# A hybrid RWKV-7 and short-convolution block: weight casts moved in a scheduler's order, splits of mixed activations spread over projection tiles

## The chip, the core and the metric

The kernel runs on one core of a Trainium2 chip. A core has five engines that take their instructions in order, each from its own stream: TensorE (PE, matrix products, with its weight loads shown as PEld), VectorE (DVE), ScalarE (ACT), GpSimd (POOL) and SyncE (SP), which here issues nearly all DMAs, one after another from one queue. The metric is the device time of one execution in microseconds; lower is better.

## What is computed

One layer of a streaming encoder over 16 meta tokens and 512 tokens of width 2048, in float32. The reference, cut to its course:

```python
hn = _rmsnorm(h_res, norm_in_g[l])
P = hn @ w_in[l]                          # 2048 -> 8320 columns
Pr, Pc = P[..., :RW_COLS], P[..., RW_COLS:]
prev = jnp.pad(Pr[:, :-1], ((0, 0), (1, 0), (0, 0)))
Pr = Pr + (prev - Pr) * mu_shift[l]       # token shift; then r, k, v, g_r, wl, al
w_raw = -jax.nn.softplus(-(w0[l] + jnp.tanh(wl) @ w_lora_up[l])) - 0.5
decay = jnp.exp(-jnp.exp(w_raw))
a = jax.nn.sigmoid(a0[l] + al @ a_lora_up[l])
# kk: k * k_k, normalised by head; k = k * (1 + (a - 1) * k_a)
y = _rwkv7_recurrence(rh, decay, kh, vh, kk, kk * ah)     # 16 heads x 64
y_a = (group_norm(y) + bonus) * jax.nn.silu(g_r)
y_b = Bg * _causal_depthwise_conv(Cg * hc, conv_w[l]) * jax.nn.silu(g_c)
h_res = h_res + jnp.concatenate([y_a, y_b], axis=-1) @ w_out[l]
out = _rmsnorm(h_res, norm_f_g)[:, N_META:]
```

## The kernel before, in words

**Precision.** Both large projections are made of three products of rounded halves: a float32 operand is split into a rounded high part (a cast on ACT) and the rest (a subtraction on DVE or POOL), and PE adds high x high, low x high and high x low. `split_w` (L123) does this to a weight quarter of 128x512: the cast of L126 on ACT (`wh`), the subtraction of L127 (`wl`), on DVE for even quarters and on POOL for odd ones. `hi` and `lo` have six buffers each, the raw weights (`wr`, 512 KB, two quarters) three. `prefetch` (L130) issues the load on SP (L134) and the two splits.

**The projection.** `plan` lists 65 tiles of 128 output columns: the low-rank tile, then for each pair of heads i its k, r, v and g, and for each channel block C, h, B and gc. `main` (L322) makes one tile from four weight quarters: 96 matmuls, or 48 of twice the width for B and gc (L314). `mains` (L448) is a generator of all tiles in turn, `use` (L376) evicts a finished tile and does what follows from it (token shift, gate, the convolution: L391 to L419, whose results for channel block i go to the DRAM tile `mixd[8 + i]`).

**The order of PE is written by hand** (L79). All other work of the recurrence is placed between projection matmuls: `fill(ns)` (L500) advances the generator by so many nominal nanoseconds, `until` (L510) until a tile is there, `step` (L491) by one matmul. The FW table (L43) holds the amounts. The other engines' orders are made by the scheduler of the language from the order of recording, dependencies and a priority; `tc.high_priority(offset=n)` makes what is recorded under it rank n places earlier. `ahead` (L532) and `low_rank` use an offset of AHEAD = 600. Stores and loads that wait for a later time are kept by `later` and issued by `run_pending`.

**A pair's preparation.** `prepare(i)` (L568) takes pair i's k, low-rank and r tiles. `low_rank` gives tz and ta (tanh on ACT); L580 adds 1 to tz on DVE, L582 is a running sum (`cc`), L584 and L586 exponentials; L589 to L609 make the operands bk and ar and the product r; L614 to L616 split a square and r (casts L550 on ACT, L551 on DVE); the gram matmuls L624 follow, masked from PSUM by L633; L653 transposes; L663 to L670 sums. Then SP stores and loads re-tiled blocks, and DVE solves 16x16 triangular blocks by many small steps (L699 to L732: `prod`, `tt`, `y`). The solved blocks are stored by L747 and loaded again by L738 and L739. `invert` (L770) joins two pairs' blocks.

**The recurrence.** `recur` (L873) walks nine chunks for all eight pairs, with projection tiles of the last channel blocks between its steps; `norm` (L950) normalises a chunk and stores it to the DRAM tile `yd`.

**The end.** `split_mix(j)` (L996) makes the two halves of mixed tile j, the left operand of the output projection. For j below 8 it loads three pieces from DRAM (L1003 to L1007), combines them on DVE (L1010, two instructions) and splits: cast on ACT (L1015), subtraction on DVE (L1016). For j of 8 and above it loads `mixd[j]` (L1014) and splits. The raw tile has four buffers, the other two pieces three each. In the kernel before, `recur` is followed by `fill(14000)`, the remaining stores, and all 16 calls in a row; for j of 8 and above, the generator is first advanced until that block's gc tile is there (L1018 to L1022). What then remains of the projection, the last B and gc tiles among it, runs to its end, and the output projection begins (L1054): four column blocks of 512, each over 16 mixed tiles and four token blocks, then residual, norm and the stores.

Of the kernel before, what the change touches and what calls it, by code (L numbers as in the profile page):

```python
# [13 lines left out]
ALU = mybir.AluOpType  # L14
# [6 lines left out]
KT = DM // P  # L21
# [6 lines left out]
NPAIR = 8  # L28
# [13 lines left out]

FW = dict(  # L43
    evac=34, start=1062, lora=2200, gram=8000, gram_b=13500, gram2=4800, gram3=3500, misc=2000, v=2000, vt=1000, solve=22500, solve_first=26000,
    tr=3200, lev=3000, cp=4200, out=1500, begin=17000, p=2900, u=2900, s=5200, last=14000,
)


AHEAD = 600


def _constants():
# [24 lines left out]
def hymba_kernel(ctx: ExitStack, tc: tile.TileContext, xt, xtok, w_in, w_out, pv, lup, cst, msk, gf, out):  # L77
    nc = tc.nc
    ctx.enter_context(tc.manual_schedule(engines={mybir.EngineType.PE}))  # L79
    cp = ctx.enter_context(tc.tile_pool(name="cp", bufs=1))  # L80
# [16 lines left out]
    def col(off, i=0):  # L97
        return pvt[:, off + i : off + i + 1]
# [24 lines left out]
    def split_w(q, rq, eng):  # L123
        hi = wp.tile([P, 512], F32R, tag="hi", name=f"wh{q}", bufs=6)
        lo = wp.tile([P, 512], F32R, tag="lo", name=f"wl{q}", bufs=6)
        nc.scalar.copy(hi, rq)  # L126
        eng.tensor_tensor(out=lo, in0=rq, in1=hi.bitcast(F32), op=ALU.subtract)  # L127
        quarters[q] = (hi, lo)

    def prefetch(upto):  # L130
        while state["next"] < min(upto, len(stream)):
            j = state["next"]
            raw = wp.tile([P, 1024], F32, tag="raw", name=f"wr{j}", bufs=3)
            state["dma"] = nc.sync.dma_start(raw, stream[j]).ins  # L134
            for q in range(2):
                split_w(2 * j + q, raw[:, q * 512 : (q + 1) * 512], nc.gpsimd if q and j > 8 else nc.vector)
            state["next"] = j + 1

    keep = ctx.enter_context(tc.tile_pool(name="keep", bufs=1, side="right"))
# [21 lines left out]
    def tr(name, dt=F32):  # L161
        return cq.tile([P, LP], dt, tag="tr", name=name, bufs=5)
# [14 lines left out]
    raw = {}  # L177
# [80 lines left out]
    with tc.issue_after(head):  # L258
        load_w(0, 1)
        load_x("gt0", 4, 4)  # L260
        load_w(1, 1)
        load_w(2, 1)
        state["next"] = 3
        load_x("gt1", 8, 4)
        for kt in range(4, 8):
            split_x(kt)
        for kt in range(4):
            square_x(kt)
        prefetch(5)
        load_x("bk", 12, 3)  # L270
        load_x("v", 15, 1)
        for kt in range(8, KT):
            split_x(kt)
            square_x(kt - 4)
        for kt in range(KT - 4, KT):
            square_x(kt)
# [4 lines left out]
    for b in range(2):  # L281
# [5 lines left out]
        out=omm, in0=pvt[:, V_MU : V_MU + 33], scalar1=-1.0, scalar2=1.0, op0=ALU.mult, op1=ALU.add  # L287
    )
    for d, off in (
# [4 lines left out]
            out=d, in0=pvt[:, off : off + 8], scalar1=0.5, scalar2=None, op0=ALU.mult  # L294
        )
    nc.vector.tensor_scalar(
        out=hv[:, 4], in0=pvt[:, V_KA : V_KA + 8], scalar1=-0.5, scalar2=1.0, op0=ALU.mult, op1=ALU.add
# [24 lines left out]
    def main(j, ranges, name):  # L322
        prefetch(2 * j + 4)
        ps = banks(ranges, name, pm, "main")
        for k4 in range(4):
            if k4 == 1:
                prefetch(2 * j + 5)
            yield from steps(ps, ranges, k4, 4 * j + k4)
        return ps
# [92 lines left out]
    ready = set()  # L422
# [62 lines left out]
    def run_pending(upto):  # L485
        while pending and pending[0][0] <= upto:
            fn = pending.pop(0)[1]
            with tc.issue_after(state["dma"]):
                fn()

    def step():  # L491
        t = next(flow, None)
        if t is None:
            run_pending(float("inf"))
        else:
            clock[0] += t
            run_pending(clock[0])
        return t

    def fill(ns):  # L500
        while ns > 0:
            seen = len(ready)
            t = step()
            if t is None:
                return
            ns -= t
            if len(ready) > seen:
                ns += FW["evac"]
# [5 lines left out]
    def low_rank(i, j, up, w0, name, pad):  # L514
        t = tr(name)
        nc.gpsimd.memset(t[:, META:CH], pad)
        hi, lo = up
        for a, b in ((0, 272), (272, L)):
            z = pz.tile([P, b - a], F32, tag="tz", name=f"{name}_{a}")
            nc.tensor.matmul(z, hi[:, j], la[:, j, a:b], start=True, stop=False)  # L520
            nc.tensor.matmul(z, lo[:, j], la[:, j, a:b], start=False, stop=True)
            with tc.high_priority(offset=AHEAD):
                if a == 0:
                    nc.scalar.activation(t[:, 0:META], z[:, 0:META], AF.Tanh, bias=w0, scale=0.5)
                    nc.scalar.activation(t[:, CH : 5 * CH], z[:, META:272], AF.Tanh, bias=w0, scale=0.5)
                else:
                    nc.scalar.activation(t[:, 5 * CH : LP], z, AF.Tanh, bias=w0, scale=0.5)
            fill(FW["lora"])
        return t


    def ahead():  # L532
        return tc.high_priority(offset=AHEAD)

    def c3(t):
        return t.rearrange("p (c s) -> p c s", s=CH)
# [31 lines left out]
    def prepare(i):  # L568
        p = i % 2
# [7 lines left out]

        tz = low_rank(i, 0, up, hv[:, 0, i : i + 1], f"tz{i}", -1.0)
        ta = low_rank(i, 1, up, hv[:, 1, i : i + 1], f"ta{i}", 0.0)
        nc.vector.tensor_scalar(out=tz, in0=tz, scalar1=1.0, scalar2=None, op0=ALU.add)  # L580
        cc = tr(f"cc{i}")
        nc.vector.tensor_tensor_scan(cc, smask.rearrange("p c s -> p (c s)"), tz, 0.0, op0=ALU.mult, op1=ALU.add)  # L582
        nc.gpsimd.memset(e1[:, :, 0:1], 1.0)
# [7 lines left out]
            out=bk[:, :, 0], in0=c3(k), scalar=hv[:, 2, i : i + 1], in1=c3(te), op0=ALU.mult, op1=ALU.mult  # L591
# [3 lines left out]
            out=ta, in0=ta, scalar1=hv[:, 3, i : i + 1], scalar2=hv[:, 4, i : i + 1], op0=ALU.mult, op1=ALU.add  # L595
        )
        nc.vector.scalar_tensor_tensor(
            out=ar[:, :, 0], in0=c3(k), scalar=col(V_KK, i), in1=e1[:, :, 0:CH], op0=ALU.mult, op1=ALU.mult
# [8 lines left out]
            out=ar[:, 1:NCH, 1], in0=c3(r), in1=e1[:, 1:NCH, 1 : CH + 1], op=ALU.mult  # L607
        )
        nc.vector.scalar_tensor_tensor(  # L609
            out=r, in0=r, scalar=hv[:, 5, i : i + 1], in1=ta[:, CH:LP], op0=ALU.mult, op1=ALU.mult  # L610
# [98 lines left out]
        def sub(x, r0, c0, dims):  # L709
            return bass.AP(tensor=x.tensor, offset=x.offset + r0 * 16 + c0, ap=[list(x.ap[0])] + dims)  # L710

        for m in (2, 4, 8):
            for b in range(16 // (2 * m)):
# [4 lines left out]
                    out=pq,  # L718
                    in0=sub(d, o, o + m, [[16, m], [0, m], [1, m]]),
# [4 lines left out]
                    out=tq.rearrange("p (i j) -> p i j", i=m), in_=pq, op=ALU.add, axis=AX.X  # L724
                )
                nc.vector.tensor_tensor(
                    out=pq,
                    in0=sub(y, o, o, [[16, m], [0, m], [1, m]]),
# [254 lines left out]
    for i in range(0, NPAIR, 2):  # L983
        invert([prepare(i), prepare(i + 1)])
    until("g", NPAIR - 1)
    ph2.close()
    with tc.tile_pool(name="ch", bufs=1, side="right", reuse_waits="tile") as ch:
        recur(ch)
        fill(FW["last"])
        run_pending(float("inf"))  # L990

    pp = ctx.enter_context(tc.tile_pool(name="pp", bufs=1, side="right", reuse_waits="tile"))
    order = list(range(KT))
    parts = {}

    def split_mix(j):  # L996
        parts[j] = [pp.tile([P, SEQ], F32R, name=f"m{a}{j}") for a in range(2)]
        mh, ml = parts[j]
        raw = pp.tile([P, SEQ], F32, tag="mraw", name=f"mr{j}", bufs=4)
        if j < NPAIR:  # L1000
            rb = pp.tile([P, SEQ], F32, tag="rb", name=f"rb{j}", bufs=3)
            gg = pp.tile([P, SEQ], F32, tag="gg", name=f"gg{j}", bufs=3)
            nc.sync.dma_start(rb, rbd[j])  # L1003
            nc.sync.dma_start(gg, gated[j])
            for h, hs, ho in heads:
                o = (h * NPAIR + place[j]) * CH
                nc.sync.dma_start(raw[hs], yd[o : o + CH])  # L1007

            for x, w, z, o in ((raw, 0, rb, ALU.mult), (raw, 1, gg, ALU.add)):
                nc.vector.scalar_tensor_tensor(  # L1010
                    out=raw, in0=x, scalar=hl[:, w, j : j + 1], in1=z, op0=o, op1=(ALU.add, ALU.mult)[w]
                )
        else:
            nc.sync.dma_start(raw, mixd[j])  # L1014
        nc.scalar.copy(mh, raw)  # L1015
        nc.vector.tensor_tensor(out=ml, in0=raw, in1=mh.bitcast(F32), op=ALU.subtract)  # L1016

    for j in order:  # L1018
        if j >= NPAIR:
            while ("gc", j - NPAIR) not in ready:  # L1020
                step()
        split_mix(j)  # L1022
    for _ in flow:
        pass
# [10 lines left out]
    last = [[pw.tile([P, 512], F32R, name=f"wlast{a}{j}") for j in range(NL)] for a in range(2)]  # L1035
# [105 lines left out]
    with tc.manual_schedule(engines={mybir.EngineType.DVE, mybir.EngineType.Activation, mybir.EngineType.Pool}):  # L1141
# [9 lines left out]
        for part in range(2):  # L1151
# [3 lines left out]
            if part == 0:  # L1155
                finish(2)
                nc.vector.tensor_tensor(
                    out=fv[:, 3, 0:1], in0=fv[:, 3, 0:1], in1=ssq[:, 3, 3:4], op=ALU.add
# [60 lines left out]
```

## Time and profile before

| | us |
|---|---|
| median of 3 runs (1066.67 to 1069.53) | 1066.87 |
| the profiled execution | 1066.87 |
| its span in the profile | 1065.1 |
| PE busy | 1040.0 |
| DVE busy | 557.2 |
| ACT busy | 367.7 |
| POOL busy | 292.4 |
| output projection begins | 877.66 |

The profile shows one execution. Lines such as L127 are those of the kernel before. A row of a timeline gives start, duration, engine, line, operation, result and operands with the shape, the count, and in brackets how long the engine stood idle just before and what ended it. A row of the chain of waits gives start, duration and what ran; the chain is followed back from the last instruction to what released each step. A row of the waits names who waited for whom, the total in microseconds, how often, and the longest. "Granted clock" is the share of TensorE's full clock that the throttle allowed.

### The profile page before, as it was taken

The page shows a single profiled execution, that of the slowest core. Times are in us where ns is not written, and L with a number is a line of the kernel's source. Part 1 is how long each engine was busy: PE and PEld are TensorE (multiplying, and loading weights), DVE is VectorE, ACT ScalarE, POOL GpSimd, SP SyncE. Part 2 cuts the span into 40 slices and gives each one's busy share as a digit, 9 for nine tenths or more (in the row PEclk, how much of TensorE's full clock was granted, in tenths as well). Part 3 has the DMA queues.
Part 4 walks back from the last instruction along what each step waited for, and adds up shares of the span by engine and source line. Part 5 has one row for each costly group of instructions (what it writes and reads, how often), then busy time and mean ns, then how long its engine had stood idle before and what let it go on. Part 6 is the DMA issues. An engine that isn't in the chain of part 4 may idle for free.

```text
span 1065.1 us, 23993 instructions
## 1 busy us (share of the span) xinstructions
PE 1040.0 (98%) x9973; PEld 950.0 (89%) x9973; DVE 557.2 (52%) x1064; ACT 367.7 (35%) x682; POOL 292.4 (27%) x307
## 2 busy tenths in 40 slices
PE   8999999999999999999999999999999899999996
PEld 6999998999998999989999989898898878888885
DVE  6784964758553767644676552355444842212132
ACT  6553422533233443233443232222222342323232
POOL 0121323223132222231222231323223142424232
PEclk9999999999999999999999999999999999999999
DMA  8455564455653366643457638676745958333314
GB/s 291 137 136 138 142 169 133 128 132 144 172 152 113 107 169 145 147 141 112 124 127 173 176 108 312 215 243 188 224 104 147 244 184 315 82 96 99 99 60 158
DMA packets 182894, 167.49 MB, mean 157 GB/s; under 512 B 120961, under 2 KB 143233, under 8 KB 182401
## 3 DMA queue, kind: packets, MB, share of 16 engines
q1 hardware_dynamic: 182208, 164.90, 54.7%
q8 instruction: 78, 1.28, 0.5%
q10 hardware_dynamic: 576, 1.07, 0.3%
q14 instruction: 32, 0.25, 0.1%
HBM read 129.05 MB, written 36.88 MB: 156 GB/s over the span
## 4 chain that ended last, share of the span: by engine, by line
PE 91%; DVE 3%; DMA 2%; issue 1%; ACT 1%; SPq 0%; POOL 0%; DVEq 0%; ACTq 0%; POOLq 0%
PE o L1054 17%; PE ps_g L314 9%; PE ps_k L314 9%; PE ps_B L314 8%; PE ps_r L314 8%; PE ps_v L314 8%; PE ps_h L314 8%; PE ps_C L314 8%; PE ps_gc L314 8%; PE g L624 2%; PE zs L932 1%; PE zy L936 1%; DVE mr L1010 1%; PE rz L887 1%; PE ps_lora L314 1%
## 5 line engine op out<-in xcount | busy, mean ns | idle before, releaser
L127 POOL TENSOR_TENSOR wl<-wr,wh 128x512 fp32r<-128x512 f32 x150 | 209.3, 1398 | 486.2 <-ACT wh L126 456.5
L126 ACT CAST wh<-wr 128x512 fp32r<-128x512 f32 x312 | 189.4, 619 | 417.9 <-PE o L1054 92.5
L127 DVE TENSOR_TENSOR wl<-wr,wh 128x512 fp32r<-128x512 f32 x162 | 119.0, 738 | 263.0 <-ACT wh L126 261.9
L1054 PE MATMUL o<-wh,m 128*128 128x512 f32 (+1 forms) x484 | 145.3, 384 | 0.0
L1054 PEld LDWEIGHTS o<-wh,m 128*128 128x128 f32 x484 | 89.6, 188 | 21.4
L1054 PE MATMUL o<-wl,m 128*128 128x512 f32 (+1 forms) x242 | 92.6, 389 | 0.0
L314 PE MATMUL ps_g<-xh,wl 128*128 128x258 f32 (+1 forms) x256 | 72.2, 282 | 4.0 <-DVE wl L127 4.0
L314 PE MATMUL ps_k<-xl,wh 128*128 128x264 f32 x256 | 73.1, 286 | 0.0
L314 PE MATMUL ps_v<-xh,wh 128*128 128x264 f32 x256 | 73.1, 286 | 0.0
L314 PE MATMUL ps_r<-xh,wh 128*128 128x258 f32 (+1 forms) x256 | 72.2, 282 | 0.8 <-ACT wh L224 0.8
L314 PE MATMUL ps_k<-xh,wh 128*128 128x264 f32 x256 | 72.9, 285 | 0.0
L314 PE MATMUL ps_h<-xh,wl 128*128 128x258 f32 (+1 forms) x256 | 72.8, 284 | 0.0
L314 PE MATMUL ps_k<-xh,wl 128*128 128x264 f32 x256 | 72.8, 284 | 0.0
L314 PE MATMUL ps_v<-xh,wl 128*128 128x264 f32 x256 | 72.7, 284 | 0.0
L314 PE MATMUL ps_v<-xl,wh 128*128 128x264 f32 x256 | 72.7, 284 | 0.0
L314 PE MATMUL ps_g<-xl,wh 128*128 128x258 f32 (+1 forms) x256 | 72.5, 283 | 0.0
L314 PE MATMUL ps_g<-xh,wh 128*128 128x258 f32 (+1 forms) x256 | 72.3, 282 | 0.0
L314 PE MATMUL ps_h<-xh,wh 128*128 128x258 f32 (+1 forms) x256 | 72.3, 282 | 0.0
L314 PE MATMUL ps_C<-xh,wh 128*128 128x258 f32 (+1 forms) x256 | 72.3, 282 | 0.0
L314 PE MATMUL ps_C<-xh,wl 128*128 128x258 f32 (+1 forms) x256 | 72.2, 282 | 0.0
L314 PE MATMUL ps_h<-xl,wh 128*128 128x258 f32 (+1 forms) x256 | 72.2, 282 | 0.0
L314 PE MATMUL ps_r<-xl,wh 128*128 128x258 f32 (+1 forms) x256 | 72.1, 282 | 0.0
(263 smaller groups left out, 2691.4 us busy)
## 6 DMA issues: line engine op xcount, KB each, us to landing
wr<-in_w_in_dram SPq DMA_DIRECT2D x127, 512.0 KB
ct<-opd SPq DMA_DIRECT2D x64, 288.0 KB
wr<-in_w_out_dram SPq DMA_DIRECT2D x32, 512.0 KB
opd<-ar SPq DMA_DIRECT2D x8, 576.0 KB
opd<-gt SPq DMA_DIRECT2D x16, 288.0 KB
opd<-bt SPq DMA_DIRECT2D x32, 128.0 KB
xres<-in_xtok_dram SPq DMA_DIRECT2D x4, 768.0 KB
out_dram<-xres SPq DMA_DIRECT2D x6, 512.0 KB
```

Of the source, the lines that this page charges most:

```text
L126: nc.scalar.copy(hi, rq)
L127: eng.tensor_tensor(out=lo, in0=rq, in1=hi.bitcast(F32), op=ALU.subtract)
L314: nc.tensor.matmul(ps[r], ww[:, w], xx[:, kt, a:b], start=(kt == 0 and n == 0), stop=(kt == KT - 1 and n == 2))
L624: nc.tensor.matmul(z[h][:, c - c0], bk[hs, c, h : h + 2, :].rearrange("p a s -> p (a s)"), ar[hs, c].rearrange("p a s -> p (a s)"), start= ...
L887: nc.tensor.matmul(z[e][ho if e else hs, 0, k], t[hs, o : o + CH], t[hs, O_V : O_V + CH] if part else st[hs, 4 * e + k], start=(part == 0 ...
L932: nc.tensor.matmul(d[hs, j], t[hs, o : o + CH], x[hs], start=(a == 0), stop=(a == b - 1))
L936: nc.tensor.matmul(d[ho, j], t[hs, o : o + CH], x[hs], start=(a == 0), stop=(a == b - 1))
L1010: nc.vector.scalar_tensor_tensor(out=raw, in0=x, scalar=hl[:, w, j : j + 1], in1=z, op0=o, op1=(ALU.add, ALU.mult)[w])
L1054: nc.tensor.matmul(ps[t + p], mm[:, tk], ww[:, o], start=(jj == 0 and q == 0), stop=(jj == KT - 1 and q == 2))
```

## The change

Four edits. The AHEAD offset goes from 600 to 3000. The two splits in `prefetch` are recorded under `high_priority(offset=1500)`. The addition of L580 moves from VectorE to GpSimd. And at the end, `split_mix` is called for tiles 8 to 11 with 3,700 nominal nanoseconds of projection after each, then, after the remaining stores, for tiles 0 to 7 with 2,600 after each, then for 12 to 15, each once its gc tile is there; before, 14,000 nanoseconds of projection stood ahead of all of them, and between them only what was still missing of a gc tile.

```diff
-    tr=3200, lev=3000, cp=4200, out=1500, begin=17000, p=2900, u=2900, s=5200, last=14000,
+    tr=3200, lev=3000, cp=4200, out=1500, begin=17000, p=2900, u=2900, s=5200, last=3700, mix=2600,
...
-AHEAD = 600
+AHEAD, WEIGHTS = 3000, 1500
...
-            for q in range(2):
-                split_w(2 * j + q, raw[:, q * 512 : (q + 1) * 512], nc.gpsimd if q and j > 8 else nc.vector)
+            with tc.high_priority(offset=WEIGHTS):
+                for q in range(2):
+                    split_w(2 * j + q, raw[:, q * 512 : (q + 1) * 512], nc.gpsimd if q and j > 8 else nc.vector)
...
-        nc.vector.tensor_scalar(out=tz, in0=tz, scalar1=1.0, scalar2=None, op0=ALU.add)
+        nc.gpsimd.tensor_scalar(out=tz, in0=tz, scalar1=1.0, scalar2=None, op0=ALU.add)
...
         recur(ch)
-        fill(FW["last"])
-        run_pending(float("inf"))
...
-    for j in order:
-        if j >= NPAIR:
-            while ("gc", j - NPAIR) not in ready:
-                step()
+    for j in range(NPAIR, NPAIR + 4):
+        split_mix(j)
+        fill(FW["last"])
+    run_pending(float("inf"))
+    for j in range(NPAIR):
+        split_mix(j)
+        fill(FW["mix"])
+    for j in range(NPAIR + 4, KT):
+        while ("gc", j - NPAIR) not in ready:
+            step()
         split_mix(j)
```

In the order of the built kernel, the number of instructions on each engine is the same but for the eight additions that change theirs; on DVE, ACT, POOL and SP some stand elsewhere. Those that the prediction speaks of are given there with their line.

## The prediction, made before the changed kernel ran

> **What bounds the kernel now.** I read the page first (engine shares, chain of waits), then who waited for whom on PE, then the timelines of the other engines wherever PE stood.
>
> ```profile
> span 1065.1 us, 23993 instructions
> ...
> PE 1040.0 (98%) x9973; PEld 950.0 (89%) x9973; DVE 557.2 (52%) x1064; ACT 367.7 (35%) x682; POOL 292.4 (27%) x307
> ...
> PE 91%; DVE 3%; DMA 2%; issue 1%; ACT 1%; SPq 0%; POOL 0%; DVEq 0%; ACTq 0%; POOLq 0%
> ```
>
> PE sets the end: it is 91% of the chain, and no other engine is busy for more than 52%. The time can only change where PE stands still, or where its clock falls. The order of PE's instructions is written by hand, and the built order of the changed kernel has PE's 7,625 instructions in the same places as before; so I ask only which waits of PE go and which come. Its waits in the body are few:
>
> ```profile
> PE ps_B L314 <- ACT wh L126: 5.8, 1, 5.8
> PE ps_g L314 <- DVE wl L127: 4.0, 3, 1.4
> ```
>
> The first is one wait of 5.8 us for the weights of the last B tile; the second is one of some 1.3 us in each of pairs 3, 5 and 7. The chain around 847 us shows why the first exists:
>
> ```profile
> 845.90 0.70 DVE m L1016
> 846.62 0.32 SPq L1014
> ...
> 846.99 0.43 SPq L419
> ...
> 847.51 5.15 DMA wr<-in_w_in_dram
> ...
> 852.76 0.63 ACT wh L126
> ...
> 853.43 13.10 PE ps_B L314 x48
> ```
>
> Columns are start, duration, work. The load of the weights was issued at 847.51, although its buffer had been free since the POOL cast that ended at 821.2: on SP's in-order queue it stood behind the loads of mixed tiles 0 to 10, each waiting for a buffer that the splits (L1010 to L1016) free one at a time, every 2.8 us. And the wait costs more than itself:
>
> ```profile
> 847.00:854.00 7.00, 1.24 (x7) 0.97 (x6) 4.71 (x9) 2.99 (x6) 1.29 (x2) 0.74 0.86 288
> 854.00:857.50 3.50, 3.50 (x10) 2.74 (x9) 3.15 (x5) 2.70 (x5) 1.25 (x1) 0.54 0.93 347
> ```
>
> The columns after the engines' busy times are the granted clock, DMA share and GB/s: 0.54 of full clock right after the wait. So this B tile took 13.10 us, while the first (at 152.60) took 11.11: another 2.0 us.
>
> The Trainium skill (TensorE: Matmul & The Clock Gate, section "What's actually happening") says that the clock halves after an idle window of about 3.4 us and returns after a busy one as long; the 0.54 agrees, and so do the three 1.3 us waits, which cost no clock (250 to 300 us: 1.00). By that rule a wait that is only shortened to under 3.4 us would already return the 2.0 us.
>
> **The change, part by part.**
>
> *Splits spread over projection tiles.* No instruction is added: 16 splits, the same loads. In the new queue the splits of tiles 8 to 11, then 0 and 1, stand ahead of the late weight load; 2 to 4 follow it, and each later weight load stands between splits. I step it with the rows of before. The four loads of 8 to 11 issue from 816.0 in 0.45 us steps; tile 0 reuses tile 8's buffer, whose split must follow the cast at 819.16 (0.62), so about 821; tile 0's load issues near 822, tile 1's near 824, the weight load at 825 instead of 847.5. With the 5.15 us of the chain it lands at 830; its cast is due when a slot frees at 833 and ends by 835, for a tile that PE begins at 847.6: 13 us spare. The later quarters wait behind the DVE/ACT chain of tiles 0 to 7, which starts at 828 (tile 0's load takes the 6.1 us of before) and runs at 2.8 us a tile plus the C and h evictions: third quarter of B cast by 848 (needed 853), first of gc by 850.5 (858.7), third of gc by 860.4 (864.3), first output weights by 863 (869.9). The smallest spare is 4 us. So the 5.8 us goes, and the 2.0 us with it: -7.8. Lower bound of the gain: 3, should the third quarter of gc come 4.8 us after PE wants it.
>
> *Weight casts ahead, three pairs.* Against the words, in pairs 3, 5 and 7 the order on ACT does not move: the five casts still follow the cast L550 of that pair. On DVE the two L127 still come after the whole solve, now even behind L551:
>
> ```profile
> 250.97 2.69 ACT L126 CAST wh<-wr 128x512 fp32r<-128x512 f32 x5
> 252.56 2.27 DVE L726 TENSOR_TENSOR prod<-y,tt 72x512 f32<-72x512 f32 x1
> 254.87 0.68 DVE L732 TENSOR_REDUCE y<-prod 72x64 f32<-72x512 f32 x1
> 255.47 1.66 DVE L127 TENSOR_TENSOR wl<-wr,wh 128x512 fp32r<-128x512 f32 x2
> ```
>
> DVE has no idle from 235.2 to 255.5 but for 0.66, and the same work stands ahead of the 255.47 row, less one L580 (0.46). L609 falls behind two solve steps (1.07 + 0.68), so ACT's five casts and POOL's start 1.8 us later; L726, stretched from 1.09 (its row at 121.42) to 2.27 by POOL's casts, may be whole again: -1.2. Against that, a new order on SP: the solved blocks' store (L747, which waits until the solve ends, 255.58) now precedes the next weight load, which had been issued at 240. It now issues near 254.5 and lands near 259.6; ACT, in order, stands at its cast until then, and the v shift behind it (258.51 before) slips to 260.6. DVE's four L633 slip from 263.1 to about 264, ending at 266.5, where PE wants their PSUM at 266.95 less what it gained. What PE gains at the first place it mostly gives back at the second. Bounds for the three pairs together: 4.0 gained (waits gone), 2.4 lost (0.8 each: L633 ending a full microsecond late). I take 0, nearest to the replayed rows.
>
> *The add to POOL* (L580, 8 times). POOL's L594, same shape, takes 0.83 alone. cc starts 0.4 later; in even pairs it has 3 us before the gram matmuls (L606 ends 208.9, PE at 212.0), so nothing there.
>
> The Trainium skill (SBUF — State Buffer, section "Who interferes with whom") says that a DVE instruction with two SBUF inputs and a GpSimd one that reads SBUF exclude each other for a whole instruction. The row agrees: an L717 of 72x8 took 1.03 at 239.19, 0.16 elsewhere, under a POOL cast of 2.44. By it, eight adds of 0.83 could hold DVE up 0.83 - 0.46 = 0.4 us each; only three of them sit ahead of a wait of PE, 1.2 us in all, inside the bounds above.
>
> *A cast that moves back.* In pair 0's conv, wl46 (row 154.02) is now behind both L404, and its ACT cast behind the L402 that waits for POOL:
>
> ```profile
> 154.02 0.68 DVE L127 TENSOR_TENSOR wl<-wr,wh 128x512 fp32r<-128x512 f32 x1
> 154.18 1.68 POOL L400 TENSOR_TENSOR u<-u,hh 128x514 f32<-128x514 f32 x1 [11.04 <-DVE hh L333]
> 155.88 0.73 ACT L402 ACTIVATE cv<-u,pvt 128x512 f32<-128x512 f32 x1 [5.66 <-POOL u L400]
> ```
>
> L402 ends 156.6; two L404 (1.01 + 0.68) end 158.4; wl46 ends 159.1. PE needs it at 152.60 + 5.55 + 0.23 = 158.4. New wait: 0.7. SP issues two more stores and one load less (about 0.5 each) ahead of that pair's solve, which can push it by up to 0.5: I take 0.8 (bounds 0 and 1.5).
>
> *The start* (34 to 42 us): the square sums L199 slip behind four casts and end near 41.4 instead of 39.4; PE wants them at 42.41. Hidden by 1 us; uncovered it would cost what it is late.
>
> **Sum.** 1065.1 - 5.8 - 2.0 + 0.8 + 0 = 1058.1 of span. The profiled execution took 1066.87, which is also the median of the three; so 1.77 lie around the span: 1059.9.
>
> **Rivals.**
> Full gain: the three waits on L127 go too and wl46 is in time: 1066.87 - 7.8 - 4.0 = 1055.1. For it: L726 shrinks. Against: five casts on ACT begin later, not earlier.
> Half a cure: the splits, now between the weight loads, delay a later quarter of the gc tile; 4 to 5 us past the spare, 3 to 4 us of wait come back: 1063.4. For it: eight tiles at 2.8 us fill DVE up to the last cast. Against: 4 us spare.
> No cure: the load stays behind the splits' buffers, as much as before: 1066.9. Against: six tiles stand ahead of it in the order, not eleven, and four of them need no DVE work before their loads but a free buffer.
> Slower: the store of L747 ahead of a weight load. ACT stands at that cast, the v shift, a cast and L633 wait behind it, and PE waits for PSUM, three times. Each microsecond that the load takes beyond 5.1 costs 3; to eat 7.8 - 0.8 and 0.3% (3.2) as well it must take over 8.5 us. The rows have 4.5 to 5.7 for such loads, 7.1 the longest (5.87 to 12.95 us). At 9: 1059.9 + 3 x 3.9 = 1071.6.
>
> **How the numbers follow.** A difference of 0.3% (3.2 us) is about what can be told from none. Forecast 0.62, full gain 0.14, half a cure 0.13, no cure 0.06, slower 0.05. Faster: 0.62 + 0.14 + two thirds of the half cure = 0.85; same: 0.06 + the rest of the half cure = 0.10; slower 0.05. The forecast with its bounds near the replay runs from 1057 to 1062; to hold 8 in 10 I reach half into the full gain and most of the half cure: 1055.8 to 1063.2.
>
> **What would show it.** In the profile after: no PE wait on wh in the last B tile and a granted clock of 1.00 throughout 840 to 880; that tile at 11.1 us. A new wait ps_B <- L127 of under 1.5 us near 158. For the pairs: the wait ps_g <- L127 shorter, and a wait of the L624 matmuls or the L653 transposes on L633 in its place. I am wrong if the last B tile still waits over 3 us, if a gc quarter does, or if the three pairs move by more than 3 us together.

## The result, and the profile after

The changed kernel takes 1060.79 us (median of 4 runs, 1059.70 to 1062.15) against 1067.07 before (4 runs, 1066.67 to 1069.53): a ratio of 0.9937, with a 95% interval from 0.9916 to 0.9958. Run a second time with five runs it took 1059.89, at 0.9934 (0.9921 to 0.9946). The profiled execution is one of 1059.78.

From here on lines are those of the changed kernel, one higher than before from L135 on (L126 and L127 stay; L1009 was L1010, L1013 was L1014), where a kernel built from it is read. Kernels that leave `split_w` as it was keep the old numbers.

The page of the profile after, span, busy times and the chain's shares:

```profile
span 1058.0 us, 23979 instructions
...
PE 1039.8 (98%) x9973; PEld 949.3 (90%) x9973; DVE 560.8 (53%) x1056; ACT 365.5 (35%) x682; POOL 306.1 (29%) x315
...
PE 90%; DVE 5%; issue 2%; DMA 1%; ACT 1%; POOL 1%; SPq 0%; DVEq 0%; ACTq 0%; POOLq 0%
```

By this page PE is busy for the same time as before (1040.0), in a span 7.1 shorter. That does not make all of the 7.1 standing, since a busy time rests on modelled ends of the matmuls: the last B tile alone took 13.10 before and takes 11.11 now. The rows below divide the difference. Who waited for whom on PE, after (total us, times, longest):

```profile
PE g L625 <- DVE gt L634: 2.2, 3, 0.8
...
PE ps_B L315 <- DVE wl L127: 1.4, 1, 1.4
PE ps_g L315 <- DVE wl L127: 0.8, 2, 0.4
PE zy L937 <- issue: 0.7, 1, 0.7
```

The wait of 5.8 us for `wh` in the last B tile is gone. The three waits for `wl` in pairs 3, 5 and 7 shrank from 4.0 in all to 0.8, and waits of the gram matmuls for `gt` (2.2) took their place. A wait of 1.4 in a B tile is new. The chain of waits and the granted clock around the last B tile, after:

```profile
836.71 11.41 PE ps_h L315 x96
848.13 11.11 PE ps_B L315 x48
859.24 0.93 PE ps_gc L315 x4
```

```profile
847.00:854.00 7.00, 7.00 (x37) 5.86 (x36) 5.73 (x8) 2.39 (x4) 4.40 (x3) 1.00 0.97 256
854.00:857.50 3.50, 3.50 (x17) 2.84 (x16) 2.78 (x5) 1.32 (x3) 0.00 (x0) 1.00 0.54 192
```

The chain is PE alone, the tile takes 11.11, and the clock stays at 1.00. SP's own queue, after, shows why: the first of these loads of weights feeds that tile, the second its second half.

```profile
827.60 0.54 SPq L134 DMA_DIRECT2D wr<-in_w_in_dram  x1
...
837.58 0.46 SPq L134 DMA_DIRECT2D wr<-in_w_in_dram  x1
```

They stand between the splits' loads now, the first 19.9 us earlier than the 847.51 of before.

A total can hide several differences, so I divide every profile at four places in PE's order, which is the same in all kernels here: the end of pair 0's B tile (the start of the first gc tile), the end of the pairs (where PE takes up a C tile again behind the first `rz` matmuls, near 652 us in the profile before), the end of the recurrence's middle (where it takes up a gc tile again behind `zy` matmuls, near 768), and the end of the last B tile (the start of the last gc tile). Lengths in us, taken from the timelines of PE:

| kernel | to pair 0's B | pairs | recurrence | to last B's end | rest |
|---|---|---|---|---|---|
| before | 163.6 | 488.4 | 116.4 | 98.0 | 198.7 |
| after | 164.8 | 489.5 | 114.5 | 90.3 | 198.9 |
| e1 splits spread only | 163.2 | 488.2 | 115.8 | 90.3 | 198.6 |
| e2 all but the splits | 165.6 | 487.7 | 116.0 | 98.2 | 198.7 |
| e3 add back on DVE | 164.2 | 488.3 | 116.5 | 90.3 | 198.7 |
| e4 after, four raw | 163.3 | 483.7 | 115.1 | 90.3 | 198.7 |
| e5 before, four raw | 163.1 | 483.6 | 114.8 | 90.8 | 198.6 |
| e6 e1, four raw | 164.0 | 483.4 | 115.7 | 90.3 | 198.7 |
| e7 no priority | 166.1 | 487.2 | 115.8 | 90.3 | 198.9 |
| e8 after again | 164.3 | 487.0 | 116.0 | 90.3 | 198.9 |
| e9 ten ahead | 163.7 | 488.7 | 116.3 | 95.4 | 198.7 |
| e10 nine ahead | 163.8 | 488.2 | 116.1 | 95.0 | 198.7 |

After minus before: +1.3, +1.0, -1.8, -7.8, +0.2. The gain is in one stretch. The experiments ask what of the rest belongs to the change, and to which of its edits.

### The profile page after: what moved, and what is told of

Same layout as the page of the kernel before. It is cut to its first block, busy times and chain, and to the rows that moved or that the text cites. A ratio compares the mean times of both kernels' runs of the same rounds, so it can differ in the third digit from the quotient of the medians.

```text
span 1058.0 us, 23979 instructions
## 1 busy us (share of the span) xinstructions
PE 1039.8 (98%) x9973; PEld 949.3 (90%) x9973; DVE 560.8 (53%) x1056; ACT 365.5 (35%) x682; POOL 306.1 (29%) x315
## 4 chain that ended last, share of the span: by engine, by line
PE 90%; DVE 5%; issue 2%; DMA 1%; ACT 1%; POOL 1%; SPq 0%; DVEq 0%; ACTq 0%; POOLq 0%
PE o L1059 17%; PE ps_C L315 9%; PE ps_gc L315 9%; PE ps_k L315 9%; PE ps_B L315 8%; PE ps_g L315 8%; PE ps_h L315 8%; PE ps_r L315 7%; PE ps_v L315 7%; PE g L625 2%; PE zs L933 1%; PE zy L937 1%; PE ps_lora L315 1%; PE rz L888 1%; DVE wl L127 1%
## 5 line engine op out<-in xcount | busy, mean ns | idle before, releaser
L127 POOL TENSOR_TENSOR wl<-wr,wh 128x512 fp32r<-128x512 f32 x150 | 208.4, 1390 | 471.0 <-ACT wh L126 433.2
L126 ACT CAST wh<-wr 128x512 fp32r<-128x512 f32 x312 | 188.7, 619 | 396.2 <-PE o L1059 93.2
L127 DVE TENSOR_TENSOR wl<-wr,wh 128x512 fp32r<-128x512 f32 x162 | 125.1, 777 | 251.9 <-ACT wh L126 249.1
```

## Experiments

The edits are told apart as: *splits* (the two loops at the end), *priority* (the `with tc.high_priority(offset=WEIGHTS)` around the casts), AHEAD 600 or 3000, and *add* (L581 on DVE or POOL). Each was timed beside the kernel before, in 3 to 5 rounds on the same chip; that took 1067.07 beside e1 to e4, 1067.23 beside e5 to e8, 1067.20 beside e9 and e10.

**e1: the splits alone.** From the changed kernel:

```diff
-AHEAD, WEIGHTS = 3000, 1500
+AHEAD, WEIGHTS = 600, 1500
...
-            with tc.high_priority(offset=WEIGHTS):
-                for q in range(2):
...
+            for q in range(2):
...
-        nc.gpsimd.tensor_scalar(out=tz, in0=tz, scalar1=1.0, ...
+        nc.vector.tensor_scalar(out=tz, in0=tz, scalar1=1.0, ...
```

> Only the splits of mixed activations are spread; AHEAD 600, no place in front for the weights' casts, the add of L580 on DVE. Theory (all of the gain is the last B tile, the other edits cost): 1067.0 - 5.8 - 2.0 = 1059.2, no wait of PE for wl at 158, the three waits ps_g <- wl L127 still about 1.3 each, none of g on gt. If the stand of 1.3 before zy that only the kernel before showed goes with the splits too, 1057.6. Rival (the casts' place in front is part of the gain): 1062 to 1064.

Measured: 1057.88 (ratio 0.9917, 0.9903 to 0.9931). Its waits of PE:

```profile
PE ps_g L314 <- DVE wl L127: 4.0, 3, 1.4
PE zy L936 <- issue: 1.7, 2, 1.1
```

The waits for `wl` are those of before, at 4.0 in three, none is at 158, none is for `gt`, and the whole last stretch is shortened by 7.7 as in the changed kernel. So all of the gain comes from the splits; the rival, 1062 to 1064, falls. The time is 1.3 below the 1059.2 of the theory; in the profile the other four stretches are 0.4, 0.2, 0.6 and 0.1 shorter than before, which is no more than they move between executions. Against the changed kernel's 1060.79 and 1059.89 the splits alone look 2 to 3 us better, but the intervals just overlap.

**e2: all the rest, without the splits.** The old loop, with `last=14000`, and the three other edits kept.

> The other way round: weights' casts in front, AHEAD 3000 and the add on POOL, but the splits as before the change. Theory: slower than before by what the new waits cost, 1067.0 + 1.7 (B tile of pair 0) + 1.0 (pairs 3, 5, 7) = 1069.7, or 1068.1 if the stand before zy goes with these edits; the wait of 5.8 for wh in the last B tile and the 0.54 of clock behind it stay. Rival (the casts in front help by themselves): 1063 to 1066.

Measured: 1067.05 against 1067.07, ratio 1.0000 (0.9987 to 1.0012).

```profile
PE ps_B L315 <- ACT wh L126: 5.7, 1, 5.7
PE zy L937 <- issue: 2.0, 2, 1.1
...
PE ps_B L315 <- DVE wl L127: 1.3, 1, 1.3
...
PE ps_g L315 <- DVE wl L127: 0.8, 2, 0.4
PE g L625 <- DVE gt L634: 0.6, 1, 0.6
```

The 5.7 is there, and so is the new wait at 158. But where the first profile of the changed kernel had 2.2 of waits for `gt`, this one has 0.6, and its pairs take 487.7, less than before. My 1068.1 to 1069.7 had added the first profile's +1.0 of the pairs as if it were the program's. It isn't. In this profile pair 0's B tile takes 1.6 more than before (12.71 against 11.11) and the pairs take 0.7 less. The rival's 1063 to 1066 falls too: these edits together are worth nothing that can be measured.

**e3: the add alone taken back** (L581 to `nc.vector`, one word).

> The changed kernel with the add of L580 back on DVE, all else changed. Theory (the order in pair 0's conv and of the blocks' store against the weight load is moved by this add, not by the casts' priority: in the built order both are as before without it): no wait at 158, no wait of g on gt, ps_g <- wl back at about 1.3 each: 1060.8 - 1.7 - 1.0 = 1058.1. Rival (the priority of the casts moves them): both waits as in the changed kernel, 1060.8.

Measured: 1059.34, ratio 0.9924 (0.9909 to 0.9938). The waits are 4.0 in three for `wl`, none for `gt`, none at 158. In the built order the places around 158 and around the blocks' store are those of before, although the casts still have their priority. So they turn with the add's move to POOL, and not with the casts' place in front. Whether the add alone would turn them with AHEAD at 600, and what AHEAD does by itself, was not run; why an add on another engine moves these places in the scheduler's order stays open. The time lies between the theory's 1058.1 and the rival's 1060.8 and does not tell them apart; the waits do.

**e7: the priority alone taken away**, AHEAD 3000 and the add on POOL kept.

> The changed kernel without the place in front for the weights' casts, all else as changed. Theory (in the built order only pair 0's conv differs by much: the cast wl46 stands between the two L404 instead of behind both): 1060.8 less up to 1.0, the wait at 158 at 0.3 to 0.9 instead of 1.4, g <- gt still three times 0.7 to 0.8. Rival (the priority brings part of the gain): 1062 to 1064.

Measured: 1060.46, ratio 0.9935 (0.9922 to 0.9949), against 0.9934 and 0.9937 with it. The priority that names the change moves the time by nothing that five rounds see. At 158 I was wrong: the wait was no shorter (1.5, for `wh`), although `wl46` now stood ahead of one of the two conv steps on DVE. Of the three waits for `gt` that I expected, one came, of 0.3.

**e8: the changed kernel once more.**

> The changed kernel once more, for what moves between two executions of one program. Theory (the waits of PE on data are the program's, the stands before zy that no instruction explains are the execution's): 1.4 at 158 and three times 0.7 to 0.8 of g on gt again; the stands before zy and the start differ by up to 1.5 from the first. Rival (the stand of 1.3 at 730 of the kernel before went with the edits): 0.7 once, as in the first profile; 1060 to 1061.

Measured: 1059.89. Two of its waits, for comparison with the first profile's:

```profile
PE zy L937 <- issue: 1.9, 2, 1.3
...
PE ps_B L315 <- DVE wl L127: 0.9, 1, 0.9
```

The theory was half wrong. The stand before `zy` did come back (recurrence 116.0, where the kernel before has 116.4), so it is the execution's. But the wait at 158 was 0.9 instead of 1.4, the waits for `gt` were gone from the list, and the pairs took 487.0 instead of 489.5 with the same program. How that can be shows in the same instructions of both executions: ACT's cast of the second weight load behind the blocks' store, DVE's subtraction, and the gram's evictions. First the first profile of the changed kernel, then this one:

```profile
256.04 2.87 SPq L134 DMA_DIRECT2D wr<-in_w_in_dram  x2
...
264.72 1.14 ACT L126 CAST wh<-wr 128x512 fp32r<-128x512 f32 x2 [2.47 <-PE ps_g L315]
...
265.38 0.69 DVE L127 TENSOR_TENSOR wl<-wr,wh 128x512 fp32r<-128x512 f32 x1 [0.89 <-ACT wh L126]
265.99 2.75 DVE L634 TENSOR_TENSOR gt<-g,cs 128x512 f32<-128x512 f32 x5
```

```profile
255.49 2.87 SPq L134 DMA_DIRECT2D wr<-in_w_in_dram  x2
...
263.52 1.26 ACT L126 CAST wh<-wr 128x512 fp32r<-128x512 f32 x2 [2.00 <-DMA wr<-in_w_in_dram]
...
264.17 0.69 DVE L127 TENSOR_TENSOR wl<-wr,wh 128x512 fp32r<-128x512 f32 x1 [0.42 <-ACT wh L126]
264.78 2.75 DVE L634 TENSOR_TENSOR gt<-g,cs 128x512 f32<-128x512 f32 x5
```

The first row of each joins two loads; from the end of their issue (258.91 and 258.36) to the cast it was 5.81 us in the one and 5.16 in the other. The gram's evictions stand behind that cast's `wl` in DVE's queue, so the difference goes through to PE, where an eviction that is 0.6 sooner is just in time. The bracket of the first cast names PE as the releaser, but the trace has the last of the load's sixteen parts done at 264.62 in the first execution, 0.10 ahead of the cast, and at 263.42 in the second, 0.10 ahead of it too: it is the load's landing. The same holds for pairs 3, 5 and 7 of all four profiles with this order (after, e2, e7, e8). In seven of these twelve cases the second load landed 5.26 to 5.45 us after its own issue, and no wait for `gt` is listed; in the other five it took 5.65, 5.95, 6.05, 6.09 and 6.18, with waits of 0.31, 0.60, 0.66, 0.75 and 0.79. The first eviction began 1.4 us after the landing in all twelve. Why a load takes 0.9 us longer in one case than in another, these traces do not show.

**e4 and e6: four raw buffers.** If late loads are behind both the waits at 158 and those in the pairs, one more buffer for raw weights should take them away without any reordering. e4 is the changed kernel with it, e6 is e1 with it. The same number is changed at the second place where this buffer is declared, for the last weights of the output projection:

```diff
-            raw = wp.tile([P, 1024], F32, tag="raw", name=f"wr{j}", bufs=3)
+            raw = wp.tile([P, 1024], F32, tag="raw", name=f"wr{j}", bufs=4)
```

> The changed kernel with four raw buffers for weights instead of three, so each load is asked for one tile earlier, and wr40 stands in front of the blocks' store. Theory (the waits of g on gt in pairs 3, 5, 7 come from a weight load behind that store, the one at 158 from a cast that is queued late): both kinds go, 1060.8 - 1.7 - 3 x 0.7 to 1.0 = 1056 to 1057. Rival (they come from DVE and POOL being late with the gram's evictions, whatever the load does): g <- gt stays at 0.7 each, 1059 to 1061.

Measured, e4: 1054.58, ratio 0.9879 (0.9863 to 0.9895), more than was expected. DVE's order in pair 3:

```profile
261.31 0.65 DVE L127 TENSOR_TENSOR wl<-wr,wh 128x512 fp32r<-128x512 f32 x1
261.88 2.47 DVE L634 TENSOR_TENSOR gt<-g,cs 128x512 f32<-128x512 f32 x4
```

The same subtraction ends 4.1 us sooner than in the first profile of the changed kernel, and the evictions with it; 1.5 of that is the first stretch, which is shorter by as much. No wait for `wl` or `gt` is left; the pairs take 483.7. Part of the gain beyond what I expected has a reason that matters for reading such lists: a wait is counted from the modelled end of the matmul before it. In the kernel before, pair 3's wait is listed at 1.41; between the starts of the two matmuls around it lie 1.69 (254.89 to 256.58) where they are 0.12 apart in a running tile, and the start behind it is 0.10 late as well: 1.67. So the three, 4.0 by the list, cost 4.8 (1.67, 1.67 and 1.45), and the pairs are 4.7 to 5.0 shorter than before with four buffers.

> Splits spread and four raw buffers; AHEAD 600, no place in front for the weights' casts, the add on DVE. Theory (with four buffers the other three edits have no wait left to move): as with all edits and four buffers, 1054.6, within 1.5, and no wait for wl or gt anywhere. Rival (the casts' place in front is worth something once the loads are early): 1056 to 1058 with waits for wl in pairs 3, 5 and 7.

Measured, e6: 1054.30, ratio 0.9880 (0.9866 to 0.9893). With four buffers the other edits are worth nothing, as the theory said.

**e5: the kernel before with four raw buffers**, and nothing else.

> The kernel before the change with nothing but four raw buffers for weights instead of three. In its built order the load of wr126 (first half of the last B tile's weights) now stands ahead of the splits' loads, and wr127 (second half) stands where wr126 stood. Theory: wr127 lands at about 852.7 and is cast by 853.4, where PE wants it at 847.6 + 5.5 = 853.1, so the wait of 5.8 shrinks to 0.3 to 1.0, which costs no clock (1.00 behind it, the tile's second half 5.6 long); ps_g <- wl (3 x 1.3) goes as in the kernel with the change and four buffers; no wait at 158: 1067.0 - 7.8 + 0.7 - 4.0 = 1056. Rival 1 (the splits' spread is needed: the wait only moves to the second half): a wait of 3 to 6 stays, 1059 to 1063. Rival 2 (any wait of PE there costs clock): 0.5 to 0.6 of clock behind the short wait.

Measured: 1054.21, ratio 0.9878 (0.9865 to 0.9892), below the 1056 that I expected. The chain around its last B tile:

```profile
841.27 3.96 DMA wr<-in_w_in_dram
...
845.33 0.63 ACT wh L126
845.96 0.02 issue
845.99 0.98 DVE wl L127
846.97 0.04 issue
847.01 5.37 PE ps_B L314 x22
```

The load that stands behind the splits is now the one for the tile's second half; it comes 0.3 late by the list and the clock stays at 1.00. The stretch to the last B's end is 90.8, against 90.3 with the splits spread. So the splits' spread and the deeper buffer cure the same wait, and the buffer cures those of the pairs too: one number changed in the kernel before is worth 13.0 us, about twice what the whole change brought, and the three versions with four buffers (1054.2 to 1054.6) cannot be told apart.

**e9 and e10: a shorter wait, for the clock.** In the kernel before, a few steps of projection are put between two splits, so that ten tiles' loads (e9, below) or nine (e10, with `j == 9`) stand ahead of the late weight load instead of eleven:

```diff
             while ("gc", j - NPAIR) not in ready:
                 step()
+        if j == 10:
+            fill(5000)
```

> The kernel before, but a few steps of projection are taken before the split of mixed tile 10, so that ten tiles' loads stand ahead of the load of wr126 instead of eleven. A tile's split takes 2.8: the load issues at 844.7 instead of 847.5 and the wait of 5.8 in the last B tile becomes about 3.0. Theory (the clock falls only behind a wait longer than some 3.4): 1.00 of clock behind it, B tile 11.1 long: 1067.1 - 2.8 - 2.0 = 1062.3. Rival (every wait of some us costs clock): 0.5 to 0.6 of clock behind it, 1064.3.

> The same with nine tiles' loads ahead. Theory (the wait is the place of one load in SP's queue, 2.8 per tile ahead of it): wait 0.2, clock 1.00, 1067.1 - 5.6 - 2.0 = 1059.5, as with the splits spread by themselves (1057.9 to 1059.3). Rival (the second half's load wr127, now behind the loads of tiles 9 to 12, is late instead): a wait of 1 to 3 in the tile's second half, 1061 to 1063.

Measured: 1064.67 (ratio 0.9979, 0.9970 to 0.9988) and 1064.83 (0.9974, 0.9963 to 0.9985). The theory missed in both. In e9 the rival came out: 1064.3, with the clock falling. In e10 no expectation did, since its rival ended at 1063. The waits were 2.9 in e9, as expected, and in e10 2.1 and 0.6 behind it, not 0.2: the load issued at 845.30 and 842.96, only 2.2 and 2.3 sooner for each tile taken from ahead of it, its first cast began 5.0 and 5.9 later, and in e10 that cast stood behind a mixed tile's on ACT. And the clock fell in both. Windows of 1 us, first of the kernel before, then e9, then e10 (the numbers behind the five engines' are the granted clock, the DMA share and GB/s):

```profile
850.00:851.00 1.00, 0.00 (x0) 0.00 (x0) 1.00 (x3) 0.10 (x1) 0.00 (x0) 0.71 0.93 317
...
857.00:858.00 1.00, 1.00 (x5) 0.85 (x4) 1.00 (x3) 0.37 (x1) 0.00 (x0) 0.88 0.95 389
```

```profile
850.00:851.00 1.00, 0.03 (x1) 0.03 (x1) 1.00 (x3) 0.70 (x2) 0.00 (x0) 1.00 0.47 76
851.00:852.00 1.00, 0.92 (x3) 0.49 (x4) 0.73 (x3) 0.96 (x2) 0.72 (x1) 0.96 0.89 336
852.00:853.00 1.00, 1.00 (x3) 0.80 (x3) 1.00 (x1) 0.09 (x1) 1.00 (x2) 0.50 0.80 229
...
855.00:856.00 1.00, 1.00 (x6) 0.78 (x5) 1.00 (x3) 0.50 (x1) 0.00 (x0) 0.83 1.01 338
```

```profile
850.00:851.00 1.00, 0.43 (x2) 0.22 (x2) 1.00 (x3) 0.47 (x1) 0.73 (x1) 0.83 0.44 166
...
854.00:855.00 1.00, 1.00 (x6) 0.83 (x5) 1.00 (x3) 0.17 (x1) 0.00 (x0) 0.96 0.56 213
```

With half speed as the lower level, a share of 0.71 in a window means that the clock was low for 0.58 of it. So it fell at 850.42 and rose at 857.24 in the kernel before, 851.92 and 855.34 in e9, 850.66 and 854.08 in e10: low for 6.82, 3.42 and 3.42. In e9 it fell while PE was already working again. So the low stretches here come in pieces of 3.4, and PE loses half of the time for which it works in them. With that the last stretch adds up in all three, against the 90.25 of the changed kernel: the kernel before is 7.78 longer (a pause of 5.91 by the starts, and half of the 3.81 from 853.43 to 857.24); e9 is 5.16 longer (3.08 of pause, 0.35 of late starts behind it, half of 3.42); e10 is 4.71 longer (2.24 and 0.72 of pauses, 0.10, half of 3.42).

## Why the prediction was right, and where it was not

The forecast was 1059.9, and the two medians are 1060.79 and 1059.89. By its own steps:

**The last B tile, -7.8: right in size and in mechanism.** The stretch went from 98.0 to 90.3, in every kernel with the splits spread. The load was stepped to 825 and issued at 827.60; the second half's cast was stepped to 848 at the latest and ran at 845.44. e1 shows that this alone is the gain, e2 that the rest has no part in it. The 2.0 for the clock was part of it, and is shown by the tile's 11.11 at 1.00.

**The new wait at 158: right in place, too small.** I took 0.8, with bounds of 0 and 1.5; the profiles list 1.4, 1.3 and 0.9, and the first stretch grew by 1.2 in the mean of three profiles of that order (164.8, 165.6, 164.3) over five of the old one (163.6, 163.2, 164.2, 163.7, 163.8). That mean still says too little: PE reached the tile no later (at 152.3 in the mean of the three, 152.6 in that of the five, so the start cost nothing), and the tile itself took 12.84, 12.71 and 12.29 in the three, and 11.11 in each of the five. So the wait cost 1.7, 1.6 and 1.2, and two of the three lie beyond the bound of 1.5. The step that failed is the length of the subtraction `wl46`. The chain of the changed kernel there:

```profile
155.57 0.73 ACT cv L403
...
156.33 0.76 DVE cv L405
...
157.78 1.78 DVE wl L127
159.56 0.04 issue
159.60 5.39 PE ps_B L315 x22
```

The two L405 ended no later than stepped; but `wl46` took 1.78 where its row before said 0.68, since in its new place POOL makes a weight subtraction beside it (from 157.45, 1.55 long, so to 159.00); from there to the end of `wl46` it is 0.56. The Trainium skill (SBUF — State Buffer, section "Who interferes with whom") says that a DVE instruction with two SBUF inputs and a GpSimd one that reads SBUF contend; the 1.78 against 0.68 agrees. An instruction that is moved must be priced with the neighbours of its new place.

**Pairs 3, 5 and 7, taken as 0: near the mean of -0.6, by more luck than the step deserved.** What PE gains at `ps_g` it does give back at the evictions L634, as foreseen, but how much varies: +1.0, -0.7, -1.3 and -1.4 against before in four profiles (after, e2, e7, e8). I had followed only the first weight load behind the blocks' store; the evictions, stepped to about 264, wait for the second one's `wl` and began at 265.99 in the first profile and at 264.78 in e8. Within the bounds of -4.0 and +2.4, and not a property that one profile can show.

**What stood in no step: the recurrence, -1.8** in the first profile. It is a stand of PE before `zy` with nothing behind it in the trace. In twelve profiles that stretch takes 114.5 to 116.5, whatever the edits; e8, the same program, had 116.0. So the first profile's 1059.78 lay so close to the forecast because +0.5 and +1.0 met -1.8.

**The reason for the two reorderings was not given.** The prediction saw in the built order that the casts' own places hardly move, against the change's words, but named no cause. e3 and e7 do in part: they come with the add on POOL, and without the priority as well.

**"A wait that is only shortened to under 3.4 us would already return the 2.0 us" is not shown, and e9 and e10 speak against reading it so.** Waits listed as 2.9, and as 2.1 and 0.6 with two matmuls between (3.08, and 2.24 and 0.72 by the starts), still cost a low stretch of 3.42. What stays true: the pauses of 1.6 by the starts, in the pairs before and at 158 after (157.78 to 159.60, less the 0.23 of a running tile), cost no clock. The Trainium skill (TensorE: Matmul & The Clock Gate, section "What's actually happening") speaks of a free-running window of some 3.4 us; the low stretches of 3.42, 3.42 and 6.82 agree with whole windows, and e9 and e10 show that one with two or three matmuls in it can still count as idle. In the 3.42 that end where the clock falls (from 848.50 in e9, from 847.24 in e10) PE stood for 2.5 and for 2.8. Where the limit lies between a pause of 1.6 and the 2.5 of e9 was not tried.

Of the rivals, half a cure and no cure fall with the 90.3. Full gain falls by the waits that came in the pairs and at 158, though e4 to e6 show that a version without them exists and ends at 1054, near the 1055.1 that the rival had worked out. The slower one needed over 8.5 us for the load behind the store. That load's cast came 4.4 after the issue (256.04 to 260.48). The second of the two, of which the rival did not speak, landed 5.3 to 6.2 after its issue and left the three pairs at most 1.0 longer, since the shorter `ps_g` wait had paid for most of it.

## What to carry to other kernels

Where several waits of the bounding engine end in the same kind of load, ask first how many buffers the loads have: one more here did what the change of order did, and 6 us more, and with it the orders that were tried could not be told apart. Test a bundle of edits one at a time, with a division of the timeline that every kernel shares: the priority, which the title names first, moved nothing that could be measured, and with an edit that looked harmless (an add to another engine) two queues turned. Take a second profile of the same program before explaining a difference of 1 us.

## What the runs showed of the hardware

The clock's low stretches around the last B tile are pieces of 3.42 us (3.42 twice, 6.82 once), and one began 0.9 us after PE had started to work again (e9: the first matmul behind the wait at 850.98, the fall at 851.92). A wait of PE listed at 1.41 was 1.67 by the starts of its instructions, so that curing three gave 4.7 to 5.0 us. And two executions of one program differ by 2.5 us in a stretch of 490 (489.5 and 487.0): three weight loads landed 6.05 to 6.18 us after their issue in the one and 5.26 to 5.39 in the other, and only the first has the three waits for `gt`, 2.2 in all. What makes PE stand before `zy` for 0.7 to 2.4 us in all, with nothing in the trace behind it, stays open.
